# Weight sums by accumulating transfers, and seven-product pairs interleaved with eight-product pairs four times a block, in a 256-token transformer block

## The chip, the cores and the metric

One NeuronCore of a Trainium2 chip runs the whole kernel. The metric is the device time of one execution in microseconds (us), taken as the median of several runs.

## The reference, cut to what matters

A transformer block on x of 256 x 2048 in float32: a norm, a mixer of four kinds of heads, an output projection, a residual, and then the feed-forward part, which is what the change touches:

```
h = rms_norm(x, norm_ffn_pre)
f = (silu(h @ w_gate) * (h @ w_up)) @ w_down      # 2048 -> 5632 -> 2048
x = x + rms_norm(f, norm_ffn_post)
```

## The kernel before, in words

Every float32 operand is split into two parts: `hi` (a cast to the type fp32r on ScalarE, L767) and `lo` (the rest, a subtraction on VectorE, L768). A product of two operands is then three matmuls, x-hi by w-hi, x-hi by w-lo and x-lo by w-hi (`mm1`, L813 to L815), each 128 x 128 by 128 x 512.

The feed-forward part takes most of the second half. Gate and up weights of columns 512 to 5632 come in ten blocks (`b` = 1 to 10) of 512 columns; a block walks over eight units `u`, each a pair of row-tiles (128 rows of the weights each). A unit has four weight tiles, called a and c (of the gate half) and b and d (of the up half), and both 128-token halves of x, that is a 2 x 2 by 2 x 2 product of tiles. `eight` computes it with eight products, `seven` with seven, in the manner of Winograd's form of Strassen's method. The seven need sums of weight tiles: `ta` = (a+b, b+d) and `tb` = (a+b+d, a+b+d+c), which VectorE makes (L824, L826, L827), and sums of x tiles (`cmb`), which are made once and kept. Before, the units 0, 2 and 4 of a block are sevens (`S_UNITS`), the other five are eights: 61 products a block. The down projection has two column halves `q` with 22 units each, of which 4 and 7 are sevens (`S_DOWN`).

Two loads of 512 KB a unit go through SP's queue into `raw` (five buffers, L793). `hi` and `lo` have four buffers each; a split therefore takes the buffer of the split four places earlier. `ta` and `tb`, the block's results `g` and `v`, the transposed activations `ft` and the split x lie in the pool `big` (34 buffers of 4 KB a partition, function `T`). The sums of a block are put together from PSUM in `sums` (the banks m1, m6, m7, q5) and `join` (the banks b2, b3, b4, b8); `turn` transposes a finished block by eight TensorE transposes; `hidden` splits what `turn` left for the down projection.

The order of the instructions on each engine's queue is set when the kernel is built, by a scheduler that goes by program order, by free buffers and by its own guess of durations; at run time each queue keeps that order, and an instruction that waits holds back all behind it on its engine.

Of the kernel before, what the change touches and what calls it, by code (L numbers as in the profile page):

```python
# [99 lines left out]
def block_kernel(ctx: ExitStack, tc: tile.TileContext, I, out):  # L100
# [15 lines left out]
    def T(shape, name, dt=F32):  # L116

        count["t"] += 1
        return big.tile(shape, dt, tag="t", name=f"{name}_{count['t']}")
# [662 lines left out]
        split_to(o[:, 0], o[:, 1], s)  # L782
        return o

    def load4(src, i):

        n = 4 * P * 512
        w = src[i * n:(i + 1) * n].rearrange("(p c n) -> p c n", p=P, c=4)
        out = []
        for k in range(2):  # L790
            raw = wp.tile([P, CK * 512], F32, tag="raw", bufs=5, name="raw")
            r3 = raw.rearrange("p (c n) -> p c n", c=CK)
            nc.sync.dma_start(r3, w[:, 2 * k:2 * k + 2, :])  # L793
# [17 lines left out]
    def mm1(m, name, xa, xb, hi, lo, last):  # L811
        o, first = bank(m, name)
        nc.tensor.matmul(o, lhsT=xa, rhs=hi, start=first, stop=False)  # L813
        nc.tensor.matmul(o, lhsT=xa, rhs=lo, start=False, stop=False)  # L814
        nc.tensor.matmul(o, lhsT=xb, rhs=hi, start=False, stop=last)  # L815

    def xpart(x, u, k, h):
        return [x[u][:, k, i, h * P:(h + 1) * P] for i in range(2)]

    def seven(m, src, i, x, u, cmb, last):  # L820

        ad, bc_ = load4(src, i)
        ta, tb = T([P, 2, 512], "ta"), T([P, 2, 512], "tb")
        nc.vector.tensor_tensor(ta, ad, bc_[:, 0:1, :].to_broadcast([P, 2, 512]), ALU.add)  # L824
        w0 = split_new(ad)
        nc.vector.tensor_tensor(tb[:, 0, :], ta[:, 0, :], ad[:, 1, :], ALU.add)  # L826
        nc.vector.tensor_tensor(tb[:, 1, :], tb[:, 0, :], bc_[:, 1, :], ALU.add)  # L827
        wa = split_new(ta)
        wc = split_new(bc_[:, 1:2, :])
        wb = split_new(tb)  # L830
        s = lambda j: [cmb[:, i, j, :] for i in range(2)]
        for name, (xa, xb), (hi, lo), k in (
                ("m1", xpart(x, u, 0, 0), w0, 0), ("b3", s(3), w0, 1), ("q5", s(0), wa, 0), ("m7", s(2), wa, 1),
                ("b2", xpart(x, u, 1, 0), wc, 0), ("m6", s(1), wb, 0), ("b4", xpart(x, u, 1, 1), wb, 1)):
            mm1(m, name, xa, xb, hi[:, k, :], lo[:, k, :], last and name[0] != "b")

    def eight(m, src, i, x, u, last=False, halves=(0, 1), ws=None):

        if ws is None:
            ws = [split_new(v) for v in load4(src, i)]  # L840
        (w0, w1) = ws
        for h in halves:
            for name, k, (hi, lo), j in (("b2" if h == 0 else "b4", 0, w0, 0), ("b3" if h == 0 else "b8", 1, w0, 1),
                                         ("b3" if h == 0 else "b8", 0, w1, 0), ("b2" if h == 0 else "b4", 1, w1, 1)):
                end = last and (name, j) in (("b3", 0), ("b8", 0), ("b2", 1), ("b4", 1)) and w1 is ws[1] and j + k == (
                    0 if name in ("b3", "b8") else 2)
                mm1(m, name, *xpart(x, u, k, h), hi[:, j, :], lo[:, j, :], end)
        return ws

    def sums(m, g, v):  # L850

# [16 lines left out]
    def combine_hs(u):  # L868
# [6 lines left out]
    accs = [[accps(f"ff{h}{i}") for i in range(2)] for h in range(2)]  # L875
    gemm(hs, [I["w_g"], I["w_u"]], [fr[0], fr[0]], 512, KT, accs, 4, (2, 3, 4, 7),
         {1: lambda: gained(1, 0), 2: lambda: gained(1, 1), 3: lambda: gained(1, 2), 4: lambda: gained(1, 3),
          5: lambda: [x_norm(h) for h in range(2)], 6: lambda: combine_hs(S_UNITS[0]),
          8: lambda: combine_hs(S_UNITS[1]), 9: lambda: combine_hs(S_UNITS[2])})
    for h in range(2):  # L880
        spill(h)
    sg = []
# [7 lines left out]
    def turn(b, f):  # L890

        ft.append(T([P, 4, S], f"ft{b}"))
        for h in range(2):
            ps = ps_c.tile([P, 512], F32, tag="b", name=f"fT{b}{h}")
# [15 lines left out]
    for b in range(1, FFB):  # L910
        m = {}
        g, v = T([P, 2, 512], "g"), T([P, 2, 512], "v")
        for u in range(KT // CK):
            i = (b - 1) * (KT // CK) + u
            if u in S_UNITS:
                seven(m, I["w_gu"], i, hs, u, cmb[u], u == S_UNITS[-1])
            else:
                eight(m, I["w_gu"], i, hs, u, u == KT // CK - 1)
            if u == 0:
                turn(b - 1, f)  # L920
            if u == S_UNITS[-1] + 1:
                sums(m, g, v)
            if u == 6 and b >= FFB - 2:
                hidden(b - FFB + 2)
# [10 lines left out]
    for q in range(2):  # L935
# [14 lines left out]
                                        g_end[:, j * 512:(j + 1) * 512], ALU.mult)  # L950

        for u in range(n_u):
            hidden(u)
            i = q * n_u + u
            if u in S_DOWN[q]:
                seven(m, I["w_down"], i, fs, u, fcmb[u], u == S_DOWN[q][-1])
# [82 lines left out]
```

## Time and profile before

| | us |
|---|---|
| median of 3 runs | 1153.43 (1153.13 to 1155.93) |
| the profiled execution | 1157.54 |
| its span, from the first to the last instruction | 1155.6 |
| TensorE (PE) busy in the span | 1123.8 (97%) |
| VectorE (DVE) busy | 865.6 (75%) |
| ScalarE (ACT) busy | 613.1 (53%) |
| GpSimd (POOL) busy | 14.2 (1%) |
| mean granted TensorE clock | 0.996 of full speed |

The span leaves out 1.9 us around the first and the last instruction. TensorE's matmuls overlap, so that one lasts 0.39 us in the records while the next begins 0.23 us after it; what a matmul costs in a row of them is the distance of the starts. The mixer and the first block of gate and up take the first 465 us, the blocks 1 to 10 the time up to about 904 us, the down projection the rest.

### The profile page before, as it was taken

What the parts mean: (1) busy time and instruction counts of PE and PEld (TensorE: products, weight loads), DVE (VectorE), ACT (ScalarE), POOL (GpSimd) and SP (SyncE); (2) the same over time, 40 slices, a digit from 0 to 9 for tenths busy, and PEclk for the clock granted to TensorE, in tenths of its full rate; (3) what the DMA queues carried; (4) which work ended last, traced back from release to release, by engine and by line L of the source; (5) the groups of instructions that cost most, each with busy time, mean ns of one, the idle gap of its engine ahead of it and who ended that gap; (6) DMA issues with size and microseconds to landing.
All of it is one profiled execution on the core that took longest, in us unless ns stands there. A gap on an engine that the chain in (4) does not pass through costs nothing. (4 is left out here: it accounts for less than half of the span.)

```text
span 1155.6 us, 14581 instructions
## 1 busy us (share of the span) xinstructions
PE 1123.8 (97%) x5341; PEld 928.8 (80%) x5341; DVE 865.6 (75%) x1185; ACT 613.1 (53%) x846; POOL 14.2 (1%) x37
## 2 busy tenths in 40 slices
PE   9999999999999999999999999999999999989996
PEld 7787888888888887887787787787788788868885
DVE  5556647777565577898898897887898988479845
ACT  6644435565444475655555555555565666355532
POOL 0000000000000010000000000000000000000000
PEclk9999999999999999999999999999999999999998
DMA  8964454564456676556556556456456556546654
GB/s 275 317 227 146 142 155 124 185 208 162 153 188 192 213 266 204 182 195 205 181 186 204 176 196 204 164 199 206 164 196 215 192 194 218 194 153 216 221 196 150
DMA packets 65447, 224.35 MB, mean 194 GB/s; under 512 B 8032, under 2 KB 8544, under 8 KB 65376
## 3 DMA queue, kind: packets, MB, share of 16 engines
q1 hardware_dynamic: 65232, 223.42, 57.9%
q8 instruction: 42, 0.69, 0.2%
q14 instruction: 29, 0.24, 0.1%
q10 hardware_dynamic: 144, 0.01, 0.0%
HBM read 219.20 MB, written 4.19 MB: 193 GB/s over the span
## 5 line engine op out<-in xcount | busy, mean ns | idle before, releaser
L767 ACT CAST hi<-raw 128x1024 fp32r<-128x1024 f32 x248 | 238.6, 980 | 205.9 <-PE b L815 180.8
L768 DVE TENSOR_TENSOR lo<-raw,hi 128x1024 fp32r<-128x1024 f32 x248 | 277.6, 1133 | 67.4 <-ACT hi L767 63.5
L182 DVE TENSOR_TENSOR lo<-raw,hi 128x1024 fp32r<-128x1024 f32 (+3 forms) x154 | 175.5, 1154 | 115.9 <-ACT hi L181 115.4
L181 ACT CAST hi<-raw 128x1024 fp32r<-128x1024 f32 (+3 forms) x154 | 150.7, 994 | 129.9 <-PE wo L199 32.1
L814 PE MATMUL b<-lo,hs 128*128 128x512 f32 x460 | 180.3, 392 | 0.3 <-DVE lo L768 0.3
L813 PE MATMUL b<-hi,hs 128*128 128x512 f32 x460 | 180.1, 392 | 0.0
L815 PE MATMUL b<-hi,hs 128*128 128x512 f32 x460 | 179.2, 390 | 0.0
L814 PE MATMUL b<-lo,fs 128*128 128x512 f32 x286 | 111.7, 391 | 0.3 <-DVE lo L768 0.3
L815 PE MATMUL b<-hi,fs 128*128 128x512 f32 x286 | 111.4, 390 | 0.0
L813 PE MATMUL b<-hi,fs 128*128 128x512 f32 x286 | 110.7, 390 | 0.1
L814 PEld LDWEIGHTS b<-lo,hs 128*128 128x128 f32 x460 | 86.4, 188 | 18.4 <-DVE lo L768 1.0
L813 PEld LDWEIGHTS b<-hi,hs 128*128 128x128 f32 x460 | 86.4, 188 | 17.8
L815 PEld LDWEIGHTS b<-hi,hs 128*128 128x128 f32 x460 | 86.4, 188 | 17.6
L824 DVE TENSOR_TENSOR ta<-raw 128x1024 f32<-128x1024 f32 x41 | 50.1, 1223 | 30.6 <-DMA raw<-in_w_gu 29.2
L814 PEld LDWEIGHTS b<-lo,fs 128*128 128x128 f32 x286 | 53.8, 188 | 12.6 <-DVE lo L768 1.4
L813 PEld LDWEIGHTS b<-hi,fs 128*128 128x128 f32 x286 | 53.7, 188 | 11.9 <-ACT hi L767 0.7
L768 DVE TENSOR_TENSOR lo<-tb,hi 128x1024 fp32r<-128x1024 f32 x41 | 50.1, 1222 | 17.1 <-ACT hi L767 17.1
L815 PEld LDWEIGHTS b<-hi,fs 128*128 128x128 f32 x286 | 53.8, 188 | 11.1
L767 ACT CAST hi<-tb 128x1024 fp32r<-128x1024 f32 x41 | 43.1, 1052 | 28.9 <-DVE lo L768 13.0
L767 ACT CAST hi<-ta 128x1024 fp32r<-128x1024 f32 x41 | 43.2, 1054 | 26.0 <-PE b L815 17.4
L768 DVE TENSOR_TENSOR lo<-ta,hi 128x1024 fp32r<-128x1024 f32 x41 | 50.0, 1219 | 0.1
L196 PE MATMUL wo<-hi,ms 128*128 128x512 f32 x128 | 50.0, 390 | 0.0
(378 smaller groups left out, 2025.8 us busy)
## 6 DMA issues: line engine op xcount, KB each, us to landing
raw<-in_w_gu SPq DMA_DIRECT2D x160, 512.0 KB, 4.5
raw<-in_w_down SPq DMA_DIRECT2D x88, 512.0 KB, 4.2
raw<-in_w_in SPq DMA_DIRECT2D x78, 512.0 KB, 4.5
raw<-in_w_out SPq DMA_DIRECT2D x32, 512.0 KB, 3.5
raw<-in_w_in SPq DMA_DIRECT2D x16, 384.0 KB, 3.1
raw<-in_w_g SPq DMA_DIRECT2D x8, 512.0 KB, 4.8
raw<-in_w_u SPq DMA_DIRECT2D x8, 512.0 KB, 4.7
raw<-in_w_in SPq DMA_DIRECT2D x8, 264.0 KB, 2.8
```

The source lines that it names most:

```text
L181: nc.scalar.copy(hi[:, k, :n], r3[:, k, :])
L182: nc.vector.tensor_tensor(lo[:, k, :n], r3[:, k, :], hi[:, k, :n].bitcast(F32), ALU.subtract)
L196: nc.tensor.matmul(d[:, :n], lhsT=a, rhs=hi[:, kt % CK, :n], start=first, stop=False)
L767: nc.scalar.copy(hi, v)
L768: nc.vector.tensor_tensor(lo, v, hi.bitcast(F32), ALU.subtract)
L813: nc.tensor.matmul(o, lhsT=xa, rhs=hi, start=first, stop=False)
L814: nc.tensor.matmul(o, lhsT=xa, rhs=lo, start=False, stop=False)
L815: nc.tensor.matmul(o, lhsT=xb, rhs=hi, start=False, stop=last)
L824: nc.vector.tensor_tensor(ta, ad, bc_[:, 0:1, :].to_broadcast([P, 2, 512]), ALU.add)
```

## The change

`fifteen` takes the place of a `seven` and the `eight` behind it: 15 products of two neighbouring units, woven so that the eight's first half stands between the seven's first two and its next two products, and the eight's second half at the end. Blocks have four such pairs (units 0, 2, 4 and 6 as sevens), 60 products; in the down projection 4 and 7 units stay sevens, at other places. The tiles of a unit are packed in the order a, b, d, c. `ta` is no longer a VectorE addition: SP loads (a, b) into it and then a transfer issued by GpSimd adds (b, d) to it in SBUF. VectorE's additions for `tb` stay, and read `ta`. A pair loads a and d (512 KB), c (256 KB, in a `raw` buffer of its own), `ta` twice 512 KB, and the eight's two times 512 KB. `turn` moves to the block's end, into the PSUM pool of the m banks; a fourth `cmb` is made in the first block of gate and up.

```
-S_UNITS = (0, 2, 4)
-S_DOWN = ((0, 1, 5, 8), (0, 1, 3, 5, 7, 8, 10))
+S_UNITS = (0, 2, 4, 6)
+S_DOWN = ((3, 7, 11, 15), (1, 3, 5, 7, 9, 11, 15))
...
-        q = np.stack([a[:, 0], b[:, 1], b[:, 0], a[:, 1]], axis=2)
+        q = np.stack([a[:, 0], b[:, 0], b[:, 1], a[:, 1]], axis=2)
...
-    def seven(m, src, i, x, u, cmb, last):
-
-        ad, bc_ = load4(src, i)
-        ta, tb = T([P, 2, 512], "ta"), T([P, 2, 512], "tb")
-        nc.vector.tensor_tensor(ta, ad, bc_[:, 0:1, :].to_broadcast([P, 2, 512]), ALU.add)
...
+    def fifteen(m, src, i, x, u, cmb, last, end=False):
...
+        ad, c_ = load4(src, i, slice(0, 3, 2), slice(3, 4))
+        n = 4 * P * 512
+        w4 = src[i * n:(i + 1) * n].rearrange("(p c n) -> p c n", p=P, c=4)
+        ta = T([P, 2, 512], "ta")
+        nc.sync.dma_start(ta, w4[:, 0:2, :])
+        nc.gpsimd.dma_start(ta, w4[:, 1:3, :], accum_op=ALU.add)
+        tb = T([P, 2, 512], "tb")
+        r0, r1 = load4(src, i + 1, slice(0, 2), slice(2, 4))
         w0 = split_new(ad)
+        prod(("m1", xpart(x, u, 0, 0), w0, 0), ("b3", s(3), w0, 1))
+        w0e = split_new(r0)
         nc.vector.tensor_tensor(tb[:, 0, :], ta[:, 0, :], ad[:, 1, :], ALU.add)
-        nc.vector.tensor_tensor(tb[:, 1, :], tb[:, 0, :], bc_[:, 1, :], ALU.add)
+        nc.vector.tensor_tensor(tb[:, 1, :], tb[:, 0, :], c_[:, 0, :], ALU.add)
+        part8(w0e)
         wa = split_new(ta)
-        wc = split_new(bc_[:, 1:2, :])
+        prod(("q5", s(0), wa, 0), ("m7", s(2), wa, 1))
+        wc = split_new(c_)
         wb = split_new(tb)
...
+        prod(("b2", xpart(x, u, 1, 0), wc, 0), ("m6", s(1), wb, 0), ("b4", xpart(x, u, 1, 1), wb, 1))
+        w1 = split_new(r1)
+        part8(w1)
...
             if u in S_UNITS:
-                seven(m, I["w_gu"], i, hs, u, cmb[u], u == S_UNITS[-1])
-            else:
+                fifteen(m, I["w_gu"], i, hs, u, cmb[u], u == S_UNITS[-1], u == KT // CK - 2)
+            elif u - 1 not in S_UNITS:
                 eight(m, I["w_gu"], i, hs, u, u == KT // CK - 1)
-            if u == 0:
-                turn(b - 1, f)
...
+        turn(b - 1, f)
         for h in range(2):
             join(m, g, v, h)
```

What that does to the queues is seen at two places. The first is SP's queue where block 2 begins. Before, every unit issued two loads, of which none is for `ta`:

```order
L793 DMA raw_4486<-in_w_gu 128x1024
L793 DMA raw_4488<-in_w_gu 128x1024
L793 DMA raw_4522<-in_w_gu 128x1024
L793 DMA raw_4524<-in_w_gu 128x1024
L793 DMA raw_4568<-in_w_gu 128x1024
L793 DMA raw_4570<-in_w_gu 128x1024
```

The last two of these are unit 0 of block 2. In the changed kernel the same queue reads as follows, where the third block begins (raw_4960 is a and d of its first pair, raw_4962 its c, raw_4968 and raw_4970 the eight's two loads; raw_5051 and raw_5053 are a and d, and c, of the second pair; ta_179 and ta_181 are the `ta` of the first and the second pair):

```order
L795 DMA raw_4857<-in_w_gu 128x1024
L795 DMA raw_4859<-in_w_gu 128x1024
L795 DMA raw_4960<-in_w_gu 128x2x512
L795 DMA raw_4962<-in_w_gu 128x512
L795 DMA raw_4968<-in_w_gu 128x1024
L795 DMA raw_4970<-in_w_gu 128x1024
L795 DMA raw_5051<-in_w_gu 128x2x512
L795 DMA raw_5053<-in_w_gu 128x512
L852 DMA ta_179_4964<-in_w_gu 128x1024
L852 DMA ta_181_5055<-in_w_gu 128x1024
L795 DMA raw_5059<-in_w_gu 128x1024
```

The first pair's `ta` stands behind the second pair's a, d and c, although the code asks for it ahead of raw_4968. So it is at the start of every block from 2 to 10; the other pairs' `ta` stand well ahead of their use.

The second place is TensorE's queue at the first pair of a block, from the first product that reads `ta` (q5). Before, in block 2, with hi_4581 and lo_4582 the parts of `ta`:

```order
L813 MATMUL q5_164_4601<-hi_4581,cmb_141_4059 128x512
L814 MATMUL q5_164_4601<-lo_4582,cmb_141_4059 128x512
L815 MATMUL q5_164_4601<-hi_4581,cmb_141_4059 128x512
L813 MATMUL m7_164_4605<-hi_4581,cmb_141_4059 128x512
L814 MATMUL m7_164_4605<-lo_4582,cmb_141_4059 128x512
```

In the changed kernel, in block 3, with hi_5005 and lo_5006 the parts of `ta`, hi_5017 of c, and hi_5021 and lo_5022 of `tb`:

```order
L815 MATMUL q5_180_5009<-hi_5005,cmb_141_4059 128x512
L815 MATMUL m7_180_5013<-hi_5005,cmb_141_4059 128x512
L815 MATMUL b2_180_4990<-hi_5017,hs_111_3717 128x512
L815 MATMUL m6_180_5028<-hi_5021,cmb_141_4059 128x512
L816 MATMUL q5_180_5009<-lo_5006,cmb_141_4059 128x512
L817 MATMUL q5_180_5009<-hi_5005,cmb_141_4059 128x512
L816 MATMUL m7_180_5013<-lo_5006,cmb_141_4059 128x512
L817 MATMUL m7_180_5013<-hi_5005,cmb_141_4059 128x512
L816 MATMUL b2_180_4990<-lo_5018,hs_111_3717 128x512
L817 MATMUL b2_180_4990<-hi_5017,hs_111_3717 128x512
L815 MATMUL b4_180_4997<-hi_5021,hs_111_3717 128x512
L816 MATMUL m6_180_5028<-lo_5022,cmb_141_4059 128x512
```

Four products are begun with their hi parts before a lo part is read. That order, q5 and m7 both by hi first, stands at ten places of the changed kernel, the first pair of the blocks 2 to 10 and the first pair of the second down half, and at one place of the kernel before, the start of the second down half.

## Rows read from the trace of the kernel before

**Rows 1.** The page's first part: busy us of an engine (share of the span) xinstructions.
```profile
PE 1123.8 (97%) x5341; PEld 928.8 (80%) x5341; DVE 865.6 (75%) x1185; ACT 613.1 (53%) x846; POOL 14.2 (1%) x37
```

**Rows 2.** Windows: the start, one block, a half-clock stretch; us, busy, PEclk, DMA share, GB/s.
```profile
0.00:50.00 50.00, 45.38 (x210) 36.40 (x211) 27.44 (x40) 31.70 (x47) 2.31 (x13) 1.00 0.86 291
596.08:639.98 43.90, 42.71 (x192) 35.01 (x191) 37.49 (x43) 24.18 (x27) 0.00 (x0) 1.00 0.58 192
1029.86:1033.28 3.42, 3.21 (x8) 2.53 (x9) 3.42 (x5) 1.41 (x3) 0.00 (x0) 0.50 0.74 219
```

**Rows 3.** Waits of PE from 480 us on: us in total, times, longest us.
```profile
PE m L814 <- DVE lo L768: 11.0, 8, 1.7
PE q L813 <- ACT hi L767: 3.1, 1, 3.1
PE b L814 <- DVE lo L768: 0.6, 2, 0.3
PE m L813 <- ACT hi L767: 0.5, 1, 0.5
```

**Rows 4.** Timeline of PE in block 3: start us, us, what [idle before <-releaser].
```profile
551.85 0.39 PE L815 MATMUL b<-hi,hs 128*128 128x512 f32 x1
552.08 0.39 PE L813 MATMUL m<-hi,hs 128*128 128x512 f32 x1
552.30 0.39 PE L814 MATMUL m<-lo,hs 128*128 128x512 f32 x1
552.53 0.39 PE L815 MATMUL m<-hi,hs 128*128 128x512 f32 x1
...
556.84 0.60 PE L896 MATMUL fT<-ident,v 128*128 128x128 f32 x4
557.19 0.48 PE L813 MATMUL b<-hi,hs 128*128 128x512 f32 x1
557.51 0.39 PE L814 MATMUL b<-lo,hs 128*128 128x512 f32 x1
```

**Rows 5.** Timeline of VectorE: three splits in a row, one addition for tb.
```profile
612.06 3.49 DVE L768 TENSOR_TENSOR lo<-raw,hi 128x1024 fp32r<-128x1024 f32 x3
615.46 0.68 DVE L826 TENSOR_TENSOR tb<-ta,raw 128x512 f32<-128x512 f32 x1
```

**Rows 6.** Timeline of PE at the start of the second down half.
```profile
1023.93 0.39 PE L813 MATMUL m<-hi,fs 128*128 128x512 f32 x1
...
1025.07 0.39 PE L815 MATMUL b<-hi,cmb 128*128 128x512 f32 x1
1028.53 0.50 PE L813 MATMUL q<-hi,cmb 128*128 128x512 f32 x1 [3.08 <-ACT hi L767]
```

**Rows 7.** Timeline of the other engines there (SPq is SP's queue).
```profile
1026.01 0.19 ACT L948 ACTIVATION_READ_ACCUMULATOR wd01j<-v 128x1 f32 x1
1026.06 0.33 SPq L937 DMA_DIRECT2D g_end<-in_g_end  x1
1026.12 1.23 DVE L824 TENSOR_TENSOR ta<-raw 128x1024 f32<-128x1024 f32 x1
1027.43 1.04 ACT L767 CAST hi<-ta 128x1024 fp32r<-128x1024 f32 x1 [1.24 <-DVE ta L824]
...
1030.52 1.22 DVE L768 TENSOR_TENSOR lo<-tb,hi 128x1024 fp32r<-128x1024 f32 x1
```

**Rows 8.** DMA issues at 598 us, at 614 us, and from 555 to 1000 us: last, us to landing.
```profile
raw<-in_w_gu SPq DMA_DIRECT2D x1, 512.0 KB, 3.1
...
raw<-in_w_gu SPq DMA_DIRECT2D x1, 512.0 KB, 5.8
...
raw<-in_w_gu SPq DMA_DIRECT2D x121, 512.0 KB, 4.5
...
g_end<-in_g_end SPq DMA_DIRECT2D x1, 512.0 KB, 7.5
```

**Rows 9.** Groups of VectorE in the block of rows 2: busy us, mean ns | idle before.
```profile
L824 DVE TENSOR_TENSOR ta<-raw 128x1024 f32<-128x1024 f32 x3 | 3.7, 1224 | 3.4 <-DMA raw<-in_w_gu 3.4
L768 DVE TENSOR_TENSOR lo<-tb,hi 128x1024 fp32r<-128x1024 f32 x3 | 3.7, 1222 | 1.1 <-ACT hi L767 1.1
```

More of the change, by code (lines that the diff above doesn't have):

```diff
@@ L783, in combine, with load4 @@
         return o
-    def load4(src, i):
+    def load4(src, i, *parts):
         n = 4 * P * 512
@@ L789, in load4 @@
         out = []
-        for k in range(2):
+        for k in parts:
             raw = wp.tile([P, CK * 512], F32, tag="raw", bufs=5, name="raw")
-            r3 = raw.rearrange("p (c n) -> p c n", c=CK)
-            nc.sync.dma_start(r3, w[:, 2 * k:2 * k + 2, :])
+            v = w[:, k, :]
+            r3 = raw[:, :v.shape[1] * 512].rearrange("p (c n) -> p c n", c=v.shape[1])
+            nc.sync.dma_start(r3, v)
             out.append(r3)
@@ L818, in xpart @@
         return [x[u][:, k, i, h * P:(h + 1) * P] for i in range(2)]
-    def seven(m, src, i, x, u, cmb, last):
-        ad, bc_ = load4(src, i)
-        ta, tb = T([P, 2, 512], "ta"), T([P, 2, 512], "tb")
-        nc.vector.tensor_tensor(ta, ad, bc_[:, 0:1, :].to_broadcast([P, 2, 512]), ALU.add)
-        w0 = split_new(ad)
-        nc.vector.tensor_tensor(tb[:, 0, :], ta[:, 0, :], ad[:, 1, :], ALU.add)
-        nc.vector.tensor_tensor(tb[:, 1, :], tb[:, 0, :], bc_[:, 1, :], ALU.add)
-        wa = split_new(ta)
-        wc = split_new(bc_[:, 1:2, :])
[L830 to L835, printed above, removed]
@@ L837, in eight @@
     def eight(m, src, i, x, u, last=False, halves=(0, 1), ws=None):
         if ws is None:
-            ws = [split_new(v) for v in load4(src, i)]
-        (w0, w1) = ws
+            ws = [split_new(v) for v in load4(src, i, slice(0, 2), slice(2, 4))]
         for h in halves:
[L843 to L847, printed above, removed]
@@ L848, in eight, with prod, part8 @@
-        return ws
+            n0, n1 = ("b2", "b3") if h == 0 else ("b4", "b8")
+            for name, k, w, j in ((n0, 0, 0, 0), (n1, 0, 0, 1), (n1, 1, 1, 0), (n0, 1, 1, 1)):
+                hi, lo = ws[w]
+                mm1(m, name, *xpart(x, u, k, h), hi[:, j, :], lo[:, j, :], last and w == 1)
+        return ws
+    def fifteen(m, src, i, x, u, cmb, last, end=False):
+        s = lambda j: [cmb[:, i, j, :] for i in range(2)]
+        def prod(*items):
+            for name, (xa, xb), (hi, lo), k in items:
+                mm1(m, name, xa, xb, hi[:, k, :], lo[:, k, :], last and name[0] != "b")
+        def part8(w):
+            k = 0 if w is w0e else 1
+            for h in range(2):
+                names = ("b2", "b3") if h == 0 else ("b4", "b8")
+                for j in range(2):
+                    mm1(m, names[j ^ k], *xpart(x, u + 1, k, h), w[0][:, j, :], w[1][:, j, :], end and k == 1)
+        ad, c_ = load4(src, i, slice(0, 3, 2), slice(3, 4))
[6 more added lines that the diff above has]
+        r0, r1 = load4(src, i + 1, slice(0, 2), slice(2, 4))
+        w0 = split_new(ad)
+        prod(("m1", xpart(x, u, 0, 0), w0, 0), ("b3", s(3), w0, 1))
+        w0e = split_new(r0)
+        nc.vector.tensor_tensor(tb[:, 0, :], ta[:, 0, :], ad[:, 1, :], ALU.add)
+        nc.vector.tensor_tensor(tb[:, 1, :], tb[:, 0, :], c_[:, 0, :], ALU.add)
+        part8(w0e)
+        wa = split_new(ta)
+        prod(("q5", s(0), wa, 0), ("m7", s(2), wa, 1))
+        wc = split_new(c_)
+        wb = split_new(tb)
+        prod(("b2", xpart(x, u, 1, 0), wc, 0), ("m6", s(1), wb, 0), ("b4", xpart(x, u, 1, 1), wb, 1))
+        w1 = split_new(r1)
+        part8(w1)
@@ L877, in block_kernel @@
          {1: lambda: gained(1, 0), 2: lambda: gained(1, 1), 3: lambda: gained(1, 2), 4: lambda: gained(1, 3),
-          5: lambda: [x_norm(h) for h in range(2)], 6: lambda: combine_hs(S_UNITS[0]),
-          8: lambda: combine_hs(S_UNITS[1]), 9: lambda: combine_hs(S_UNITS[2])})
+          5: lambda: [x_norm(h) for h in range(2)], **{c: (lambda u=u: combine_hs(u)) for c, u in zip((6, 8, 9, 10), S_UNITS)}})
     for h in range(2):
@@ L893, in turn @@
         for h in range(2):
[L894 removed]
+            ps = accps(f"fT{b}{h}")
             for j in range(4):
@@ L915, in block_kernel @@
             if u in S_UNITS:
[L916 to L917 removed]
+                fifteen(m, I["w_gu"], i, hs, u, cmb[u], u == S_UNITS[-1], u == KT // CK - 2)
+            elif u - 1 not in S_UNITS:
                 eight(m, I["w_gu"], i, hs, u, u == KT // CK - 1)
[L919 to L921 removed]
+            if u == 4 and b == FFB - 1:
+                hidden(0)
+            if u == S_UNITS[-1]:
                 sums(m, g, v)
[L923 to L924 removed]
+        turn(b - 1, f)
         for h in range(2):
@@ L960, in block_kernel @@
                 held[u] = eight(m, I["w_down"], i, fs, u, u == n_u - 1, halves=(0,))
-            if q == 0 and u == 1:
+            if q == 0 and u == 0:
                 turn(FFB - 1, f)
-            if u == S_DOWN[q][-1] + 1:
+            for k in (u + 1, u + 2):
+                if k < n_u:
+                    hidden(k)
+            if u == S_DOWN[q][-1]:
                 g, v = T([P, 2, 512], "g"), T([P, 2, 512], "v")
```

5 lines of the change are left out of this document (3 added, 2 removed).

## The prediction

> **What bounds the kernel now.** I read the page's busy shares first: TensorE is busy 97% of the span, VectorE 75%, GpSimd 1% [rows 1]. Then one block of gate and up in the windows: 43.90 us long, TensorE busy 42.71, VectorE 37.49, the DMA engines 0.58 of the time at 192 GB/s [rows 2]. So the feed-forward part runs at TensorE's rate, with VectorE not far behind and DMA with room. The waits of TensorE show what little it loses: 11.0 us in 8 waits of an m product for a lo part, and 3.1, 0.6 and 0.5 us more, 15.2 us together [rows 3]. The first kind is one wait a block; there VectorE's additions for `ta` had waited for their loads (3.4 us in the block of rows 2) [rows 9]. Last I read the timeline at the 3.1 us wait, since it is the nearest thing in this trace to what the change makes: at the start of the second down half TensorE ran out of work at 1025.07 and got q5 at 1028.53, when `ta`, which VectorE began only at 1026.12, had been cast [rows 6, 7]. Right behind it the granted clock was 0.50 for 3.42 us, 8 matmuls long, that is the lower of its two levels (1.2 of 2.4 GHz) [rows 2].
>
> **What it removes.** Ten blocks lose one product each (61 to 60), the down projection none (11 sevens before and after). A product is three matmuls at 0.227 us from start to start (0.68 us from 551.85 to 552.53) [rows 4]: 10 x 0.68 = **6.8 us** off. The 41 additions for `ta` (1.22 us each [rows 9]) leave VectorE, some 50 us of work, but VectorE is beside TensorE, so this counts only by the waits that it ends. I let all of them go: 15.2 us [rows 3], and 1.6 us of the half-clock stretch (8 matmuls in 3.42 us, at full pace 8 x 0.227 = 1.8) [rows 2]. Together 6.8 + 16.8 = **23.6 us** off. The transposes of `turn` move and stay as many: 0.35 us for four and 0.09 more for the matmul behind them [rows 4], 0.9 a block. The fourth `cmb` falls into the first block of gate and up, where TensorE waits for nothing; were it not covered, it would cost some 2 us once. Packing in another order, and c in a load of its own, I cost at nothing: the loads of `raw` are a pair or more ahead, and SP's 0.33 us an issue [rows 7] are spread over 10 us a pair; if they come late, the splits of the next pair are late.
>
> **What it adds.** A wait for `ta`, and at ten places I think nothing hides it. Look at the two orders in the section on the change. `ta` of a block's first pair stands on SP's queue behind c of the second pair. That load needs the sixth `raw` buffer of five, and gets the one that the first eight's load had, when its lo part is done. Its hi part in turn needs the buffer of c's hi part in the block before's last pair. So I count from the moment, call it zero, at which TensorE has done c's product there. What follows on each side:
>
> - The load: VectorE makes lo of a and d, one sum of 0.6 and lo of the eight's load, 1.14 each ((3.49 - 1.22) / 2) [rows 5], the first of them from 0.4 on (its cast, 1.04 [rows 7], starts three matmuls before zero): done at 3.3. SP issues c, then `ta`: 3.6. It lands after 4.5 us, the median [rows 8]: 8.1.
> - The accumulating transfer: GpSimd waits for the landing and issues it, 0.33 us as on SP: 8.4. No row shows an accumulating transfer or one from GpSimd. From below, a plain load of the same size with nothing in flight before it lands in 3.1 us; from above, the slowest one seen in the stage took 7.5 [rows 8]; a gain is excluded, as nothing can be read before it has landed. I take 5.8, the load that had another in flight [rows 8], for it reads its destination too and the second pair's `ta` is in flight right before it. **`ta` is ready at 14.2.**
> - VectorE and ScalarE then make `tb` (two additions), the hi and the lo parts of `ta`, c and `tb`. In the place of rows 7 this took from 1027.35 (end of `ta`) to 1031.74 (end of lo of `tb`): 4.4 us. So m6 can read `tb`'s lo at 18.6.
> - TensorE without a wait: by its order 18 matmuls to the block's end, eight transposes, 18 matmuls to q5 and 11 to m6's lo: 47 x 0.227 + 0.9 = 11.6 us. It has to wait 18.6 - 11.6 = **7.0 us**.
>
> Behind VectorE's waiting addition stand all its other splits, so TensorE has nothing else to do; the loads behind it on SP wait for the same addition to free a and d. After the wait TensorE's pace returns with half-clocked matmuls, at least the 1.6 us of rows 2. That is 8.6 us at each of the blocks 2 to 10 (block 1 has its `ta` loaded early): 9 x 8.6 = 77.4 us. At the second down half `ta` stands behind the last use of the old g: in rows 7 that ended at 1026.20, 2.3 us after the second half's first matmul at 1023.93 [rows 6, 7]; with a load of g_end before it `ta` is issued at 2.7, ready at 2.7 + 4.5 + 0.33 + 5.8 = 13.3, and m6's lo could start at 53 x 0.227 = 12.0: 13.3 + 4.4 - 12.0 = 5.7, and 1.6, **7.3 us**. The second to fourth pairs have 20 us and more from issue to use, against the 15 that load, accumulation and splits take; there I add nothing, and nothing for the first down half (17 us).
>
> **The sum.** 1157.5 - 23.6 + 77.4 + 7.3 = 1218.6 against the profiled execution's own time. The median of the runs lies 4.1 us under that one (1153.4), so I forecast **1214 us**, 5.3% slower.
>
> The ends: with 3.1 us for both transfers and no half clock, `ta` is ready at 10.1, the wait is 2.9 in each block and 1.6 in the down half: 27.7 in all, and 1157.5 us. With 5.8 for the load and 7.5 for the accumulation it is ready at 17.2; 10.0 us of waiting and two half-clock stretches are 13.2 a block, 11.9 in the down half, 130.7 in all, and 1260 us.
>
> A page bears on the unknown price. The rows give 3.1 us for 512 KB with an empty queue, 5.8 with one load ahead [rows 8]. The Trainium skill, "DMA: Bandwidth & Descriptors", section on the anatomy of a GpSimd-issued transfer, gives about 2 us fixed and the bytes at 436 GB/s, 3.2 us for this size, the same as the rows with an empty queue and less than those with something in flight; it gives no time for an accumulating one. By that figure for both transfers the sum would come to an estimated 1175 us, still slower.
>
> **The rivals.**
> - *In time after all, and faster.* If `ta` is ready by 7.2, nothing waits, and 1157.5 - 23.6 - 4.1 = 1130 us. For it: GpSimd is idle and its queue is empty [rows 1], DMA has room [rows 2], and VectorE loses 50 us of work. Against it: from the issue at 3.6 both transfers would have to land in 3.6 us, where one alone takes 3.1 [rows 8]. The change breaks even where the wait is 23.6 / 10 = 2.4 us, `ta` ready at 9.6; two empty-queue loads one after the other miss that by 0.5. Chance 0.10.
> - *Once and not again.* The wait of the first block might leave the loads ahead for all later ones: 1130 + 8.6 + 7.3 = 1146 us. Against it: the load's place is tied to TensorE's progress by the buffers anew in each block. Chance 0.03.
> - *DMA fills up.* A block moves 16 x 0.524 = 8.4 MB before, and 4 x 2.88 = 11.5 MB after, 37% more; if the accumulation moves its bytes twice, 13.6 MB. At 0.58 for 192 GB/s that would be 0.94 of the DMA engines in a block of the old length, more than the 0.86 of the kernel's first 50 us [rows 2]. It decides if blocks come near their old length, since then every load lands late: with 7.5 us for both transfers `ta` is ready at 18.9, 11.7 + 3.2 = 14.9 us at ten places, 1279 us. In the longer blocks that I forecast (about 50 us) even 13.6 MB is 272 GB/s, 0.82. The Trainium skill's section "Issuing engines are not separate DMA queues" on the same page says that transfers of all issuing engines share the same 16 DMA engines, which is what this rival needs; no row here shows it for GpSimd. Chance 0.07.
> - *It doesn't do what it says:* the products fall by ten in the built order, so this is only open for `ta` standing early; the order shows it late. I give it no chance of its own.
>
> **How the numbers follow.** The forecast has 0.80, the rivals 0.10, 0.03 and 0.07. A measurement of this kernel can tell 0.3%, 3.5 us, from no change. Faster by more than that are the first two rivals: 0.13. Within it lies only a thin piece of the forecast's low end, 0.02. Slower: 0.85. The range takes in the two ends of the unknown prices but for their last few us, 1163 to 1258; the two faster rivals and most of the third lie outside, and are the 2 in 10.
>
> **What would show it.** In the profile of the changed kernel: blocks 2 to 10 each with one wait of PE for hi of `ta` of about 6 us at q5, and a shorter one at m6; VectorE's addition for `tb` waiting for the GpSimd transfer in all of them; stretches of clock 0.50 behind; blocks of about 50 us against 43.9; the m waits of rows 3 gone. The accumulating transfers should take 4 to 7 us to land. I am wrong if that addition hardly waits at the block starts, if blocks come under 43.9 us, or if the waits stand at other pairs, in which case the loads as a whole are late and not this one.

## The result, and the profile after

The changed kernel takes 1280.87 us (median of 4 runs, 1275.90 to 1285.80) against 1153.89 us for the kernel before beside it: ratio 1.110, 95% interval 1.105 to 1.115. Forecast were 1214 us, range 1163 to 1258: the direction holds, the size is about double. The profiled execution took 1275.90 us, its span is 1274.1, so the two profiled spans differ by 118.5 us.

The page of the changed kernel: the busy times, GpSimd's DMA queue (packets, MB, the time of its packets as a share of 16 engines) and the issues of `ta` (the last column is the median time to landing).

```profile
PE 1150.1 (90%) x5311; PEld 940.6 (74%) x5311; DVE 852.5 (67%) x1190; ACT 629.4 (49%) x867; POOL 58.9 (5%) x88
...
q0 software_dynamic: 7344, 26.74, 12.1%
...
ta<-in_w_gu SPq DMA_DIRECT2D x40, 512.0 KB, 5.7
ta<-in_w_gu POOLq DMA_DIRECT2D x40, 512.0 KB, 6.7
```

TensorE fell from 97% to 90% of a longer span [rows 1], VectorE from 75% to 67%. In us VectorE got no busier (852.5 against 865.6). TensorE did, by 26.3 us (1150.1 against 1123.8), although it has 30 matmuls fewer: matmuls behind a wait run at the lower clock (see the half clock below). Most of the rest is waiting. What TensorE and then VectorE waited for, from 455 us to the end (us in total, times, longest):

```profile
PE q L815 <- ACT hi L768: 69.1, 11, 7.8
PE b L816 <- DVE lo L769: 23.2, 9, 5.1
PE m L816 <- DVE lo L769: 13.1, 11, 3.6
PE b L815 <- ACT fs L768: 1.8, 1, 1.8
PE q L816 <- DVE lo L769: 0.9, 1, 0.9
```

```profile
...
DVE tb L859 <- DMA ta<-in_w_gu: 95.4, 25, 6.8
DVE tb L859 <- DMA ta<-in_w_down: 38.7, 5, 9.7
```

Against the 15.2 us of before [rows 3] it is now 106.3 (without the 1.8 us for `fs` at the start of the down projection, which the kernel before has not, and e7 below has without any transfer). One part stands at q5, the first product that needs `ta`; the other part (23.2, 13.1 and 0.9) stands at lo parts inside the blocks and in the down projection. Behind most of it VectorE's `tb` addition waits for a transfer into `ta`. One of the longer blocks, of 56.77 us (columns: PE, PEld, DVE, ACT, POOL busy, clock, DMA share, GB/s), where before it was 43.90 [rows 2]:

```profile
559.93:616.70 56.77, 46.83 (x192) 37.45 (x189) 38.11 (x47) 25.83 (x30) 3.49 (x4) 0.88 0.72 205
```

Both kinds of wait are in the timeline of block 2: its beginning and, from 523 us on, its third pair. The rows are of TensorE, then SP's queue, GpSimd's and VectorE.

```profile
502.04 0.39 PE L817 MATMUL b<-hi,hs 128*128 128x512 f32 x1
...
518.41 0.79 PE L815 MATMUL q<-hi,cmb 128*128 128x512 f32 x1 [6.92 <-ACT hi L768]
...
538.81 0.50 PE L816 MATMUL m<-lo,hs 128*128 128x512 f32 x1 [1.39 <-DVE lo L769]
...
542.80 0.39 PE L815 MATMUL q<-hi,cmb 128*128 128x512 f32 x1
...
505.86 0.34 SPq L795 DMA_DIRECT2D raw<-in_w_gu  x1
506.25 0.90 SPq L852 DMA_DIRECT2D ta<-in_w_gu  x2
...
523.31 0.59 SPq L852 DMA_DIRECT2D ta<-in_w_gu  x1
...
511.85 0.87 POOL L853 DMA_DIRECT2D ta<-in_w_gu  x1 [29.30 <-DVE cs L780]
...
528.62 0.87 POOL L853 DMA_DIRECT2D ta<-in_w_gu  x1 [14.67 <-PE b L817]
...
505.75 0.68 DVE L874 TENSOR_TENSOR g<-v,m 128x512 f32<-128x512 f32 x1
...
509.94 1.41 DVE L947 SCALAR_TENSOR_TENSOR v<-v,rsf_r,g 128x512 f32<-128x512 f32 x2
...
517.25 0.69 DVE L859 TENSOR_TENSOR tb<-ta,raw 128x512 f32<-128x512 f32 x1 [4.98 <-DMA ta<-in_w_gu]
...
536.93 0.69 DVE L859 TENSOR_TENSOR tb<-ta,raw 128x512 f32<-128x512 f32 x1 [3.46 <-DMA ta<-in_w_gu]
537.54 2.35 DVE L769 TENSOR_TENSOR lo<-raw,hi 128x1024 fp32r<-128x1024 f32 x2
```

Zero of the forecast, the end of c's product, is at 502.43 (502.04 and 0.39). SP issues c at +3.4 and `ta` at +3.8, GpSimd issues the accumulating transfer at +9.4, and VectorE can read `ta` at +14.8. Forecast were 3.3, 3.6, 8.4 and 14.2, so this chain runs as it was forecast, and TensorE waits 6.9 us where 7.0 was forecast.

Two things in these rows were not in the forecast. From 505.75 to 511.3 VectorE works off the sums of the finished block in one piece (L874 to L947, of which the first and the last row stand above), so up to there it could not have made `tb` either. It is through with that before `ta` comes, so here the transfers set the wait and not the piece. And in the third pair, at 536.93, the addition waits again, with two lo parts behind it, the first of which TensorE then waits for. VectorE came to that addition at 533.47 (536.93 - 3.46), 10.2 us after SP had issued the load of this `ta` (523.31), while q5 follows only at 542.80, 19.5 us after it. The load took 5.3 us to GpSimd's issue (528.62) and the accumulation 8.3 more, 13.6 together. So "well ahead of their use", as the section on the change has it for these pairs, does not hold: the use that counts is the addition, since in VectorE's queue it stands ahead of the lo parts of the pair's own first products.

### The profile page after: what moved, and what is told of

It is laid out like the page before. It is cut to its first block, busy times and chain, and to the rows that moved or that the text cites. A ratio compares the mean times of both kernels' runs of the same rounds, so it can differ in the third digit from the quotient of the medians.

```text
span 1274.1 us, 14817 instructions
## 1 busy us (share of the span) xinstructions
PE 1150.1 (90%) x5311; PEld 940.6 (74%) x5311; DVE 852.5 (67%) x1190; ACT 629.4 (49%) x867; POOL 58.9 (5%) x88
## 3 DMA queue, kind: packets, MB, share of 16 engines
q0 software_dynamic: 7344, 26.74, 12.1%
## 4 chain that ended last, share of the span: by engine, by line
PE 56%; DMA 22%; DVE 11%; issue 7%; ACT 3%; SPq 0%; POOL 0%; POOLq 0%; DVEq 0%; ACTq 0%
DMA ta<-in_w_gu 15%; PE b L816 6%; PE b L815 6%; PE b L817 6%; DVE lo L769 6%; DMA ta<-in_w_down 5%; PE sx L223 2%; PE wo L200 2%; PE wo L197 2%; PE wo L198 2%; DMA raw<-in_w_gu 2%; PE dk L223 2%; ACT hi L768 2%; PE lk L223 2%; PE rqk L223 2%
## 5 line engine op out<-in xcount | busy, mean ns | idle before, releaser
L768 ACT CAST hi<-raw 128x1024 fp32r<-128x1024 f32 (+1 forms) x248 | 234.5, 962 | 216.2 <-PE b L817 168.7
L769 DVE TENSOR_TENSOR lo<-raw,hi 128x1024 fp32r<-128x1024 f32 (+1 forms) x248 | 270.2, 1110 | 83.0 <-ACT hi L768 79.4
L816 PE MATMUL b<-lo,hs 128*128 128x512 f32 x400 | 160.7, 402 | 14.5 <-DVE lo L769 14.5
L815 PE MATMUL b<-hi,hs 128*128 128x512 f32 x400 | 160.3, 401 | 0.0
L817 PE MATMUL b<-hi,hs 128*128 128x512 f32 x400 | 157.3, 397 | 0.0
L859 DVE TENSOR_TENSOR tb<-ta,raw 128x512 f32<-128x512 f32 x51 | 35.2, 690 | 138.2 <-DMA ta<-in_w_gu 95.4
L768 ACT CAST hi<-ta 128x1024 fp32r<-128x1024 f32 x51 | 53.5, 1049 | 126.1 <-DMA ta<-in_w_gu 82.3
L815 PEld LDWEIGHTS b<-hi,hs 128*128 128x128 f32 x400 | 78.3, 196 | 17.7
L817 PEld LDWEIGHTS b<-hi,hs 128*128 128x128 f32 x400 | 77.5, 194 | 16.5
L815 PE MATMUL q<-hi,cmb 128*128 128x512 f32 x51 | 24.0, 471 | 69.1 <-ACT hi L768 69.1
L769 DVE TENSOR_TENSOR lo<-tb,hi 128x1024 fp32r<-128x1024 f32 x51 | 62.3, 1221 | 25.3 <-ACT hi L768 25.3
L816 PEld LDWEIGHTS b<-lo,fs 128*128 128x128 f32 x286 | 54.5, 190 | 21.3 <-DVE lo L769 9.9
L768 ACT CAST hi<-tb 128x1024 fp32r<-128x1024 f32 x51 | 53.7, 1052 | 32.5 <-DVE tb L860 17.6
L769 DVE TENSOR_TENSOR lo<-ta,hi 128x1024 fp32r<-128x1024 f32 x51 | 62.1, 1218 | 8.9 <-ACT hi L768 8.9
L815 PEld LDWEIGHTS q<-hi,cmb 128*128 128x128 f32 x51 | 10.6, 207 | 75.3 <-ACT hi L768 73.8
L815 PEld LDWEIGHTS b<-hi,fs 128*128 128x128 f32 x286 | 54.4, 190 | 14.2 <-ACT fs L768 2.0
```

The costliest lines, as they stand in the source:

```text
L768: nc.scalar.copy(hi, v)
L769: nc.vector.tensor_tensor(lo, v, hi.bitcast(F32), ALU.subtract)
```

## The experiments

The edits are against the changed kernel unless said otherwise. "Gate and up" in the table is the time from the first product of block 1 to the first product of the down projection, "down" from there to the start of the last matmul, both from the timelines of the profiled executions. Spans are of one execution each. The runs of e8 alone lie far apart (1177.89 to 1191.58 us) and its profiled one is the slowest of them, so differences with e8 are given between the medians too.

| kernel | median us | ratio to before (95%) | span | gate and up | down |
|---|---|---|---|---|---|
| before | 1153.89 | 1 | 1155.6 | 438.8 | 240.6 |
| the change | 1280.87 | 1.110 (1.105 to 1.115) | 1274.1 | 535.3 | 264.3 |
| e1: VectorE sums `ta`, interleaved | 1193.76 | 1.035 (1.031 to 1.039) | 1190.8 | 474.5 | 240.3 |
| e4: second transfer plain | 1227.10 | 1.062 (1.060 to 1.065) | 1225.6 | 495.2 | 255.7 |
| e5: no second transfer | 1156.79 | 1.001 (0.999 to 1.003) | 1153.3 | 442.8 | 236.4 |
| e6: VectorE sums in first pairs only | 1248.17 | 1.081 (1.079 to 1.082) | 1247.9 | 514.7 | 257.7 |
| e7: e1 with three pairs | 1146.95 | 0.992 (0.989 to 0.995) | 1145.1 | 428.8 | 239.3 |
| e7b: the same at units 1, 3, 5 | 1148.53 | 0.993 (0.991 to 0.995) | 1146.6 | 431.6 | 240.1 |
| e8: both transfers from GpSimd | 1185.59 | 1.025 (1.019 to 1.030) | 1189.8 | 454.8 | 252.7 |
| e2: transfers in the order of before | 1326.80 | 1.147 (1.142 to 1.152) | 1322.4 | 566.1 | 280.2 |
| e10: e8 with three pairs | 1169.70 | 1.013 (1.011 to 1.015) | 1167.8 | 430.7 | 255.8 |
| e11: the change with three pairs | 1239.55 | 1.073 (1.070 to 1.077) | 1235.0 | 501.2 | 259.3 |
| e12: before with a fourth seven | 1201.47 | 1.040 (1.038 to 1.043) | 1199.9 | 480.8 | 244.8 |
| e13: e8, second transfer plain | 1173.36 | 1.016 (1.013 to 1.019) | 1172.6 | 445.8 | 244.1 |

**The interleave without the transfers (e1).**

```
-        ad, c_ = load4(src, i, slice(0, 3, 2), slice(3, 4))
+        ad, bc_ = load4(src, i, slice(0, 3, 2), slice(1, 4, 2))
+        c_ = bc_[:, 1:2, :]
...
-        nc.sync.dma_start(ta, w4[:, 0:2, :])
-        nc.gpsimd.dma_start(ta, w4[:, 1:3, :], accum_op=ALU.add)
+        nc.vector.tensor_tensor(ta, ad, bc_[:, 0:1, :].to_broadcast([P, 2, 512]), ALU.add)
```

> The interleave of the change stays, but both rows of `ta` are summed by VectorE as before, from the two ordinary loads, so no transfer writes `ta`. Theory A (the two transfers into `ta`, one after the other, cost the time, by TensorE's waits): the waits of TensorE at q5 (69.1 us in the changed kernel) and for lo parts behind VectorE's waiting addition (about 36 us) go, with most of the 20 us of half-clocked matmuls; the ten products stay away; 1281 - 69 - 36 - 20 = 1156 us or less, down to 1153 - 6.8 - 11 = 1135 us if before's m waits go too. Rival D (the interleaved order itself, with five `raw` buffers, makes the waits): over 1200 us, with q and m waits at the pairs' starts. Which one of these it is also shows whether the interleave alone is worth having.

1194 us is between the two: 83.3 us of span go with the transfers, but 35.2 above the kernel before stay, where by theory A it should have come out level with that or under it. TensorE's waits in this kernel:

```profile
PE q L815 <- ACT hi L768: 19.5, 9, 2.2
PE m L815 <- ACT hi L768: 13.2, 9, 1.5
```

They stand at the nine block starts, and the timeline of one shows why:

```profile
611.35 0.50 PE L815 MATMUL q<-hi,cmb 128*128 128x512 f32 x1 [2.18 <-ACT hi L768]
...
613.91 0.57 PE L815 MATMUL m<-hi,cmb 128*128 128x512 f32 x1 [1.55 <-ACT hi L768]
...
603.43 0.68 DVE L874 TENSOR_TENSOR g<-v,m 128x512 f32<-128x512 f32 x1
...
607.62 1.41 DVE L947 SCALAR_TENSOR_TENSOR v<-v,rsf_r,g 128x512 f32<-128x512 f32 x2
608.95 1.22 DVE L853 TENSOR_TENSOR ta<-raw 128x1024 f32<-128x1024 f32 x1
```

With the last pair at unit 6, `sums` (L873 to L876) can only begin at the block's end, and there stands in one piece with `join` and the multiplications behind SiLU; the next block's `ta`, here an addition of VectorE, comes after them, at 608.95. In the kernel before, the last seven is at unit 4, and the next block's `ta` is made ahead of `join`:

```profile
584.26 0.68 DVE L856 TENSOR_TENSOR v<-q,g 128x512 f32<-128x512 f32 x1
...
587.51 1.23 DVE L824 TENSOR_TENSOR ta<-raw 128x1024 f32<-128x1024 f32 x1 [1.15 <-DMA raw<-in_w_gu]
...
593.98 0.68 DVE L860 TENSOR_TENSOR g<-g,b 128x512 f32<-128x512 f32 x1
```

**The second transfer as a plain copy, and left out (e4, e5).** In e4 `accum_op=ALU.add` is dropped; in e5 the line of the second transfer:

```
-        nc.gpsimd.dma_start(ta, w4[:, 1:3, :], accum_op=ALU.add)
```

> The second transfer into `ta` is an ordinary copy from GpSimd's queue in place of an accumulating one; `ta` is then (b, d) and not the two sums (the additions a+b and b+d are left out). Its place, its wait for the first transfer and its bytes stay. Theory A (late place in the queue and two transfers in series): the chain is nearly as long, so 1250 to 1280 us; q waits of 5 to 7 us in blocks 2 to 10 stay. Rival C (accumulation itself is what is slow, since the destination has to be read too): the transfer lands in about 4.5 us where the accumulating one took 5.4 to 8.3, in-block waits go, and the time falls to 1200 us or less.

> The second transfer into `ta` is left out altogether; `ta` is then (a, b) and not the sums (the additions of b and d are left out). The place of the first one on SyncE's queue stays. Theory A with two links in series: `ta` is ready at about 8.1 to 8.6 us after zero instead of 14.7, the q waits fall from about 7.5 to 1.5 us or less each and the lo waits inside the blocks go: 1130 to 1160 us. Rival E (the late place of the first load alone is enough to stop TensorE): over 1200 us with q waits of 4 us and more. Rival B (DMA engines full): it moves 20 percent less than the changed kernel, about 1180 to 1220 us, with all loads faster to land.

Neither theory has e4 alone. Of the 120.8 us of span between the change and e5, 48.5 go with accumulation and 72.3 with the second link of the chain (between the medians 53.8 and 70.3 of 124.1). In e5 the first load still stands at its late place, and hardly matters (the two big waits of the change fell to these in e4 and e5):

```profile
PE q L815 <- ACT hi L768: 50.1, 10, 6.1
PE b L816 <- DVE lo L769: 8.6, 5, 2.8
PE m L816 <- DVE lo L769: 5.5, 6, 2.5
```

```profile
PE q L815 <- ACT hi L768: 8.9, 9, 2.4
PE q L816 <- DVE lo L769: 2.6, 10, 0.4
```

In e4 the lo waits inside the blocks and the down projection shrink most, from 23.2 and 13.1 to 8.6 and 5.5: there the accumulating transfer itself came late. The q waits fall less, from 69.1 to 50.1. On the page of e4 the same packets of the second transfer cost the DMA engines half:

```profile
q0 software_dynamic: 7344, 26.74, 6.6%
```

6.6% x 16 DMA engines x 1225.6 us / 7344 is 0.18 us a packet; in the changed kernel 12.1% x 16 x 1274.1 / 7344 is 0.34.

**VectorE's sums in the first pairs alone (e6).** `if u < 2:` the loads and the sum of e1, otherwise the two transfers.

> As the changed kernel, but in the first pair of each block of gate and up, and of the second down half, VectorE sums `ta` as before; the other 29 pairs keep their two transfers. Theory A: the q waits at the blocks' first pairs (63 us) and at the second down half (6 us) go with about half of the half-clock excess, and the lo waits inside the blocks (m products of the third pair, b products of the fourth, about 36 us) stay, for there the accumulating transfers land late: 1195 to 1215 us. Rival B (the DMA engines are too full, so that all loads are late): little is gained, 1245 us or more, since three quarters of the extra bytes stay. Rival F (the lo waits inside the blocks were only a consequence of the block's late start, which bunches its loads): they go too, 1130 to 1160 us.

The time is rival B's (1245 us or more), and A's and F's are missed; but e8 below speaks against B's reason. The waits tell what happened: with `ta` from VectorE, the q waits end as in e1 and not at nothing, and inside the blocks the waits grew (from 36.3 to 53.7):

```profile
PE b L816 <- DVE lo L769: 29.1, 9, 4.9
PE m L816 <- DVE lo L769: 24.6, 10, 5.2
PE q L815 <- ACT hi L768: 19.3, 9, 2.2
```

So about a third of the wait saved at the first pair (17.4 of 49.8 us) is lost again at the next ones. That their transfers then have that much less time is a reading that was not tried. Theory F, by which these waits should go, falls. (40 pairs keep their transfers here, not 29 as was written beforehand.)

**Three pairs, VectorE's sums (e7, e7b).** e1 with `S_UNITS = (0, 2, 4)`, and with `(1, 3, 5)`.

> As the run in which VectorE sums `ta` in the interleaved order, but with three such pairs a block (units 0, 2 and 4) in place of four, so one product more a block; `sums` then stands before the last two eights and not at the block's end. In that run nine additions of `sums` and `join` and the two multiplications behind SiLU stand in a row on VectorE ahead of the next block's `ta` (603.43 to 608.95 us), and TensorE waited 2.2 and 1.5 us there. Theory G (the fourth pair is what puts these together; it costs by itself): the q and m waits at the blocks' starts (32.7 us) go, with most of the 14 us of extra half clock: 1194 + 7 - 33 - 12 = 1156 us, give or take 6. Rival D (the interleaved order itself): the waits stay, 1190 to 1205 us.

> As before it with three pairs a block, but at units 1, 3 and 5, so that a block begins and ends with an eight (12 products that need no sums) and the additions of `join` have these to hide behind. Theory G: no waits at the blocks' starts, 1145 to 1158 us, at or a little under the kernel before. Rival D: the waits move to the new first pairs, 1165 us or more.

Theory G holds, and e7 comes out 3 us under its range: 45.7 us of span less than e1 although TensorE has a product more a block, and 0.8% faster than the kernel before. The waits of e7 (and 1.8 us for `fs`):

```profile
PE m L816 <- DVE lo L769: 2.0, 4, 0.7
PE b L816 <- DVE lo L769: 1.8, 3, 0.8
```

None is left at q5. This is the best version found, with e7b level with it: the interleave of the change and what goes with it (the packing, the moved `turn`, the other units in the down projection), without its other two parts.

**The fourth seven alone (e12).** The kernel before with `S_UNITS = (0, 2, 4, 6)` and a fourth `cmb`, and nothing else.

> The kernel before with a fourth seven a block (unit 6) and nothing else: ten products fewer, VectorE's sums, no interleave, no transfers. Theory G: `sums` and `join` stand together at the block's end here too, so waits of 3 to 4 us at the blocks' starts eat the 6.8 us: 1165 to 1195 us. If the fourth pair is harmless without the interleave: 1145 to 1150 us.

Theory G again, without the interleave, and 6 us over its range: ten products less and 44.3 us more span. The waits at the blocks' starts:

```profile
PE q L814 <- DVE lo L768: 30.4, 10, 3.1
PE m L814 <- DVE lo L768: 12.4, 11, 1.7
```

What e1 and e12 can't tell apart is the place of the piece and VectorE's work as a whole. Over gate and up of e12 (columns as in the window of the result):

```profile
463.53:944.36 480.83, 440.99 (x1882) 355.36 (x1880) 415.13 (x480) 258.76 (x292) 0.00 (x0) 0.96 0.53 175
```

VectorE works 41.5 us a block there (411.8 / 10 = 41.2 in e1), and 60 products at full pace with the transposes are 60 x 0.68 + 0.9 = 41.7 of TensorE: with a fourth seven and its own additions for `ta` VectorE has next to no room. In the changed kernel, without these additions, it works 37.1. The next two runs show what the place does by itself.

**The first load from GpSimd too (e8), and with three pairs (e10).**

```
-        nc.sync.dma_start(ta, w4[:, 0:2, :])
+        nc.gpsimd.dma_start(ta, w4[:, 0:2, :])
```

> As the changed kernel, but the first load of `ta` is issued by GpSimd too, so that neither of the two stands behind the `raw` loads on SyncE's queue; each is still followed by the accumulating one. Theory A in its part on the place in the queue: `ta` is issued as soon as its buffer is free, and the q waits at the blocks' starts fall from 7 us to at most the 3.7 us of waiting that VectorE's work at a block's end makes by itself; the lo waits inside the blocks fall too if they come from late issue: 1195 to 1225 us. Rival C with the shared DMA engines (accumulating transfers take 6.7 us and more wherever they are issued, and GpSimd now works off pair after pair in a row): little is gained or the chain grows, 1260 us or more.

> Interleaved, three pairs a block (units 0, 2, 4), and both transfers into `ta` issued by GpSimd: the two things together that each took most of the loss away. If the places of loss are the queue place and the bunched sums and nothing else, no large wait is left, and VectorE is lighter by the `ta` additions than in the three-pair run with VectorE's sums (1147 us): 1135 to 1150 us. Rival C (accumulating transfers cost by their length and by filling the DMA engines even when early): 1160 us or more, with lo waits behind `tb`.

e8 is 84.3 us of span under the changed kernel with the same transfers (95.3 between the medians), and 9 us under the range given: the place in SP's queue was most of what made them late. The rest of its q waits in gate and up is VectorE's piece at the block's end: `ta` is there, and `tb` and the lo part of `ta` stand right behind the piece, whose last row (L947) starts at 569.69. The waits of TensorE, and that `tb` in one block:

```profile
PE q L816 <- DVE lo L769: 18.6, 9, 2.6
PE b L816 <- DVE lo L769: 10.4, 4, 5.8
PE q L815 <- ACT hi L768: 5.0, 1, 5.0
...
571.95 0.68 DVE L859 TENSOR_TENSOR tb<-ta,raw 128x512 f32<-128x512 f32 x1
```

So the place costs by itself: these 18.6 us of waits stand behind the piece although VectorE works only 37.0 us a block (369.6 / 10). The fourth pair as a whole, its transfers included, is 22.0 us of span from e10 to e8 (15.9 between the medians), against 45.7 where VectorE also makes `ta` (e7 to e1).

e8 also decides the rival that the DMA engines are full. Over gate and up it keeps them busier and moves more than the changed kernel does (0.74, 213 GB/s), and is faster:

```profile
471.27:926.11 454.84, 430.82 (x1882) 350.55 (x1880) 369.60 (x430) 257.36 (x288) 51.98 (x73) 0.98 0.84 249
```

e10 missed its 1135 to 1150 us and came out in rival C's range, but without that rival's waits in gate and up. Gate and up is as short as in e7 (430.7 and 428.8 us), so there the transfers are hidden but win nothing over VectorE's sums. Of the 22.7 us of span between them 16.5 are in the down projection (255.8 and 239.3). On GpSimd's queue one wait stands out there, for a buffer of `ta`, and what follows it are accumulations in series:

```profile
POOL ta L852 <- ACT wd01j L966: 74.4, 1, 74.4
POOL ta L853 <- DMA ta<-in_w_down: 45.0, 6, 10.0
```

That these waits cause the 16.5 us was not tried.

**The order of before with the transfers (e2), and the change with three pairs (e11).** e2 is the old order with three sevens, its `ta` made by the two transfers; e11 is the change with `S_UNITS = (0, 2, 4)`.

> The order of the kernel before (seven, then eight, three pairs a block, VectorE's sums in their old place), with `ta` made by the load and the accumulating transfer: the transfers without the interleave and without the fourth pair. Theory A (late place, two in series): a load of `ta` stands behind c's load again in two of three pairs a block, so waits of several us at q5 in most blocks: 1200 to 1260 us. Theory G alone (the fourth pair and its bunched sums cost the time, the transfers by themselves little): 1150 to 1170 us.

> The changed kernel with three pairs a block in place of four, the transfers where the change puts them. If the transfers' place and the bunched sums add up, this takes the part of the sums away (about 40 us in the runs with VectorE's sums, 1194 to 1147) and leaves the late transfers: 1225 to 1250 us. If the late transfers alone set every wait and the sums were hidden behind them, it stays at 1265 to 1290 us; if the two eights at a block's end give the next block's `ta` the time that it lacked, it falls to 1150 to 1190 us.

e2 is worse than theory A said: 1327 us, the slowest of all. By the code a seven there needs `ta` two products after it starts, without the eight's half in between; that this is the cause was not tried. e11 came out as said (1240 us), and the two costs nearly add: the fourth pair is 39.1 us of span with the transfers (1274.1 to 1235.0) and 45.7 without. Where the transfers are early it is 22.0 (above).

**Accumulation when the transfer is early (e13).** e8 with the second transfer as a plain copy.

> As the run in which GpSimd issues both transfers into `ta` (1186 us), but the second is an ordinary copy, so `ta` is (b, d) and the additions a+b and b+d are left out. If accumulation costs only where the transfer is late: 1175 to 1190 us, with the waits that remain from the block's end. Rival C (accumulation costs by itself): 1165 us or less.

1173 us, between the two theories and just under the range of the first: accumulation is 17.2 us of span here (12.2 between the medians) and was 48.5 at the late place (change to e4). It costs mostly by making a late chain longer, but not only by that.

## Why the prediction was wrong, point by point

Between the spans the change costs 118.5 us; 61.1 were forecast (84.7 added, 23.6 removed), so 57.4 are missing. TensorE's own record says where they stand. Its waits grew by 92.9 us (106.3 and 1.8 for `fs`, against 15.2), and 53.5 were forecast (68.7 against 15.2): 39.4 missing, of which 37.2 are lo waits. Ten products, 6.8 us, did go, and yet it was busy 26.3 us longer, so the matmuls that stayed took 33.1 us longer; 14.4 were forecast, all of it half clock (10 x 1.6 - 1.6): 18.7 missing. These two are 58.1, the missing 57.4 to within 1 us.

- **The wait at q5: right, mechanism and size.** The chain to `ta` (14.2 forecast, 14.8 measured) and the q waits (9 x 7.0 + 5.7 = 68.7 forecast, 69.1 measured in 11, of which one of 1.7 stands in the first down half and was not forecast) came as worked out, link by link.
- **The other pairs: this step failed, and it is most of the miss.** "The second to fourth pairs have 20 us and more from issue to use, against the 15 that load, accumulation and splits take; there I add nothing, and nothing for the first down half". Lo waits of 37.2 us stand inside the blocks and in the down projection (23.2, 13.1 and 0.9). The distance to q5 was about right (19.5 us in the third pair of block 2 above). But VectorE comes to the `tb` addition there 10.2 us after the issue, and while it waits it holds back the lo parts behind it, which the pair's first products need; load and accumulation took 13.6, where 10.6 had been forecast (4.5, 0.33 and 5.8).
- **The half clock: mis-sized.** 1.6 us a wait was too little, and TensorE waits 33 times (11 + 9 + 11 + 1 + 1), not ten. The three windows around the q wait of block 2 are the gap's beginning, the stretch at half clock and what follows:

```profile
507.10:516.03 8.93, 4.38 (x21) 3.32 (x19) 5.14 (x11) 2.32 (x4) 1.74 (x2) 1.00 0.78 194
516.03:522.86 6.83, 4.45 (x10) 3.24 (x11) 5.39 (x6) 3.91 (x5) 0.00 (x0) 0.50 0.87 232
522.86:532.00 9.14, 9.14 (x41) 7.56 (x41) 6.52 (x7) 5.03 (x6) 0.87 (x1) 1.00 0.84 259
```

  TensorE idled from 511.5 until 518.41, the clock fell to its lower level (1.2 of 2.4 GHz) 2.4 us before that and stayed there for 4.45 us of matmuls, ten of them, where a full-speed row needs 10 x 0.227 = 2.3: 2.2 us lost, not 1.6. The mean granted clock is 0.960 over the whole kernel, where it was 0.996. That all of the 33.1 us is half clock was not added up wait by wait.
- **What it removes: the fourth pair was booked with the wrong sign.** The waits of before did go with the interleave: e7 is 10.5 us of span under the kernel before, for 16.8 forecast. But "Ten blocks lose one product each" is true and worth nothing here: the fourth pair costs 39.1 us of span in the change (e11 to the change), 45.7 with VectorE's sums (e7 to e1) and 44.3 by itself (e12). It carries `sums` to the block's end, ahead of the next block's `tb` and splits on VectorE. The prediction read VectorE's work over a block (37.49 of 43.90 us [rows 2]) and never looked at the piece that it has to do between the last m product and the next q5. In the change this is no third loss beside the two above: from e11 to the change the q waits grow by 24.6 us (44.5 to 69.1), which the prediction had, and the lo waits by 15.9 (21.3 to 37.2), which it had not.
- **By the edits.** From the kernel before to the changed one: the interleave with three pairs -10.5 (before to e7), the fourth pair +45.7 (e7 to e1), the transfers +83.3 (e1 to the change); together +118.5. In the other order the transfers come first, +89.9 (e7 to e11), and the fourth pair is +39.1. That 83.3 lies so near to the 84.7 forecast as added is luck: e1 still has VectorE's additions for `ta` and 32.7 us of waits behind them at the block starts (19.5 and 13.2). In e5, where `ta` needs neither these nor a second transfer, 11.5 us are left at q5 (8.9 and 2.6), and it is 2.3 us of span under the kernel before, not 23.6.
- **The transfer's time.** Forecast 5.8 us for the accumulating transfer; the median in gate and up was 6.7 (page above). Of the range's ends, 3.1 and 7.5, the upper one was near.
- **The rivals.** *In time after all* fell: at q5 `ta` is late in all of the blocks 2 to 10. *Once and not again* fell: nine blocks wait alike. *DMA fills up* fell by e8. Its number, 1279 us, is that of the result by chance; its mechanism is not. *It doesn't do what it says* stays closed. The page of the Trainium skill that the prediction cited, "DMA: Bandwidth & Descriptors", section on the anatomy of a GpSimd-issued transfer, would have 3.2 us for 512 KB and an estimated 1175 us; the rows of this kernel have 6.7 for an accumulating transfer and 4.4 for the plain one in e4, both with others in flight, so for both the measured numbers decide.
- **The signs named beforehand.** q waits at blocks 2 to 10: yes. Blocks of about 50 us: 53.5 on average (535.3 / 10). Landings of 4 to 7: at the upper end, with a median of 6.7 in gate and up. "If the waits stand at other pairs, in which case the loads as a whole are late": a third of the waiting does, yet the loads of `raw` still landed in 4.3 us (512 KB, median); what came late there were the transfers into `ta`.

## What to carry to other kernels

When an edit moves the last producer of a block, add up what each in-order engine has to do between that point and the next block's first need, for this is not seen in its busy share over a whole block. When an operand comes late, look at what stands behind its first reader in that engine's queue, and not only at the product that needs it: here the lo parts of other products stood there. A transfer that depends on another transfer belongs on a queue on which nothing unrelated stands ahead of it: here the same two transfers cost 84 us less of span from a queue of their own. Try the parts of a change one at a time: here one part of three was worth 0.8%, and the other two hid it.

## What the runs showed of the hardware that had not been expected

- A packet of an accumulating transfer holds a DMA engine 0.34 us where a plain one from the same queue, of the same size, holds it 0.18 (change and e4). Landing took 6.7 us against 4.4 in the median. (From GpSimd's queue alone, with both kinds in it, a packet took 0.25 us in e8, and 0.17 with plain ones only in e13.)
- GpSimd's issue of such a transfer took 0.87 us on its engine (row 511.85), where 0.33 was forecast as on SP; a plain one in its place took 0.54 (e4).
- From one queue, transfers into `ta` landed in 7.2 us in the median (e8, both kinds together, gate and up) although VectorE did not wait for them there: a slow transfer that is early cost less here than a faster one that was late.
